# A gathered-row stream whose planner cost per half-step goes from 1.65 to 1.9

## The chip, the cores and the metric

The kernel runs on one core of a Trainium2 chip. The metric is the device time of one execution in microseconds (us); the median of the runs is compared. The program is one launch; its arrays are laid out on the host beforehand.

## The reference, cut to what matters

One layer of a streaming encoder is applied to 1024 prompt frames and to 32 frames of a running stream. After a mixer (attention and a recurrence) comes PEER, a retrieval of single-neuron experts:

```
q    = x @ w_q                            # 8 heads, two halves each
e    = top-16 of 16384 experts per head   # from two top-16 lists of 128 keys
gate = softmax(the 16 scores)
hid  = gelu(down[e] . x)                  # 8 heads x 16 experts = 128 per frame
y    = x + sum over the 128 of gate * hid * up[e]
out  = rmsnorm(y)
```

So every frame needs 128 rows of `down` and 128 rows of `up`, each of 1024 floats, chosen by its own data.

## The kernel before

The frames are cut into tiles of 128: tiles 0 to 7 of the prompt and a tile "S" of the 32 stream frames. The experts are computed in two ways.

The **dense way** takes tiles 0 to 4 (640 frames). It computes all 16384 experts as matrix products: 128 blocks of 128 experts, called e here. `hidden(e)` multiplies a block of `down` (line 261 to 263, three partial products for precision, in two chunks of 320 columns), ScalarE applies the gelu, VectorE multiplies by the gates (`gated`, L1211, from a matrix that the stream `scatter` has written to DRAM) and splits the product into a high and a low part (`vwl`, L255). The products with `up` follow four blocks later; VectorE adds their results into `acc` (L1274). The loop of `stage_v` has 128 steps, each with one `hidden` and `gated` (of the block four ahead) and two blocks of columns of the product with `up`.

The **row way** takes tiles 5, 6, "S" and 7 in this order, in the stream `rows`. For each of 128 + 128 + 32 + 128 = 416 columns of chosen experts, GpSimd starts a gather of 128 rows of 2048 floats, 1 MB, into one of five buffers (L1044); VectorE multiplies by x and sums (L1047); ScalarE does the gelu and the gate on one number per frame (L1049, L1050); VectorE adds gate times `up` row onto a PSUM tile (L1031). A tile ends with a norm and a store.

The two ways, and the streams `attn`, `routing` (the top-16 searches and gates) and `scatter`, are Python generators that emit instructions. **The weave** of their instructions is made by a planner at the end of `step_kernel`: each stream has a clock, and the stream with the lowest clock emits next and moves its clock on by what it yields. `rows` yields `GC` twice for each column, `stage_v` a fixed cost for each step:

```python
                late.append((k, row))
                yield GC
                if len(late) > 1:
                    add(*late.pop(0))
                yield GC
...
                    yield 6 * KD * n / 2400.        # stage_v, one step: n = 640, KD = 8
```

`v_start`, which opens the pools of the row stream, costs 10 x 1.0 for transposes and 6 x `3 * KD * NV / 2400.` for the first six `hidden` ahead of `stage_v`, whose own first six yields are 1.0 each. While the dense stage runs, the planner also sets a limit on how far ahead of the dense stream the rows may be put on VectorE (`PACED`, `AHEADS = dict(rows=60.0)`; `marks` holds, for each planner call of the dense stream, its clock and its last VectorE instruction):

```python
        if PHASE[0] in PACED.get(x[0], ()):
            due = x[2] - AHEADS.get(x[0], 0.0)
            hold = next((m for v, m in reversed(marks) if v <= due), None)
        with tc.issue_after(hold) if hold else nullcontext():
```

Within a stretch that is held in this way, a VectorE instruction of the row stream stands behind the VectorE instruction `hold` in VectorE's order; GpSimd's and ScalarE's are not held by it. The order that the planner writes is a priority: the framework that orders each engine's queue may still put an instruction that is ready ahead of an earlier one that isn't, within the dependencies and the holds. Each engine then works through its queue in order.

Of the kernel before, what the change touches and what calls it, by code (L numbers as in the profile page):

```python
# [50 lines left out]

GE = 6

GC, SC = 1.65, 1.0

PACED = dict(rows=(1, 2), routing=(0, 1, 2))
AHEADS = dict(rows=60.0)
# [1390 lines left out]
```

## Time and profile before

| | |
|---|---|
| median of 3 runs | 3603.99 us (3594.76 to 3604.02) |
| the profiled execution | 3604.3 us |
| its span, first to last instruction | 3602.5 us |
| TensorE matmuls busy | 3259.8 us (90%) |
| TensorE weight loads busy | 3135.7 us (87%) |
| VectorE busy | 2834.6 us (79%) |
| ScalarE busy | 1614.2 us (45%) |
| GpSimd busy | 2018.5 us (56%) |
| mean granted TensorE clock | 0.952 of full |

In the profile PE is TensorE, PEld its weight loads, DVE is VectorE, ACT ScalarE, POOL GpSimd, SP the queue that starts plain DMAs; L1047 is line 1047 of the kernel. Matmuls are pipelined and their ends are modelled, so counts of matmuls per stretch say more than their busy time. A mean of one instruction is in ns, all other times in us from the start of the span.

### The profile page before, as it was taken

Reading aid. Unit: us, or ns where it says so; the run is one execution under the profiler, and the core shown is the slowest. Engines: PE = TensorE matmul, PEld = TensorE weight load, DVE = VectorE, ACT = ScalarE, POOL = GpSimd, SP = SyncE. Lnnn points to the kernel's source line nnn. Section 1 sums busy time; section 2 is a strip of 40 time slices with the busy share of each in tenths; the row PEclk is TensorE's granted clock in tenths of the full one; section 3 lists DMA queues with packets and bytes.
Section 4 is the critical chain, followed back from the end, with each engine's and each line's share of the span. In section 5 each row is a group of like instructions: output and inputs, shape, how many; then the busy total and the mean of one; then the engine's idle time right before and its main releaser. Section 6 shows DMA issues by size and latency. Waiting matters only on the chain.

```text
span 3602.5 us, 60487 instructions
## 1 busy us (share of the span) xinstructions
PE 3259.8 (90%) x21635; PEld 3135.7 (87%) x21635; DVE 2834.6 (79%) x6148; ACT 1614.2 (45%) x4034; POOL 2018.5 (56%) x1339
## 2 busy tenths in 40 slices
PE   7999899989988888774899888999999999999997
PEld 6989899877877887774899888999999999999997
DVE  3354468898678999988999999888888888788833
ACT  3544344456777747763333333333333333333322
POOL 2322224546334556565666569666766676677633
PEclk9999999999988999886999999999999999999999
DMA  4554364444565635489888778999889898999832
GB/s 163 167 159 149 109 206 167 158 138 149 173 191 161 227 123 153 139 321 343 307 318 323 299 269 312 356 338 359 314 324 355 300 355 324 346 336 351 298 109 94
DMA packets 357453, 881.01 MB, mean 245 GB/s; under 512 B 31008, under 2 KB 190240, under 8 KB 299808
## 3 DMA queue, kind: packets, MB, share of 16 engines
q1 hardware_dynamic: 297248, 440.91, 36.9%
q0 software_dynamic: 59904, 436.23, 31.8%
q8 instruction: 171, 2.80, 0.3%
q14 instruction: 130, 1.06, 0.1%
HBM read 784.47 MB, written 92.14 MB: 243 GB/s over the span
## 4 chain that ended last, share of the span: by engine, by line
PE 57%; DVE 28%; DMA 4%; issue 4%; ACT 3%; POOL 2%; SPq 0%; DVEq 0%; ACTq 0%; POOLq 0%
PE gv L261 12%; PE gv L262 11%; PE gv L263 11%; PE gm L261 6%; PE gm L263 6%; PE gm L262 6%; DVE row L1047 5%; DVE xp L1031 5%; DVE acc L1274 2%; DVE oh L967 2%; PE ws L1093 1%; DVE ohB L1132 1%; DVE ef L972 1%; PE gb L468 1%; DMA row<-in_p_rows_dram,ei 1%
## 5 line engine op out<-in xcount | busy, mean ns | idle before, releaser
L261 PE MATMUL gv<-vwh,uh 128*128 128x320 f32 x2048 | 648.3, 317 | 96.7 <-DVE acc L1274 63.9
L255 POOL TENSOR_TENSOR wl<-wr,wh 128x1024 fp32r<-128x1024 f32 x160 | 390.4, 2453 | 540.7 <-ACT wh L254 524.9
L261 PE MATMUL gv<-vxh,dh 128*128 128x320 f32 x2048 | 643.9, 315 | 21.7 <-DVE acc L1274 10.2
L1044 POOL DMA_INDIRECT row<-in_p_rows_dram,ei x384 | 514.3, 1339 | 259.1 <-DVE xp L1031 141.7
L263 PE MATMUL gv<-vxh,dl 128*128 128x320 f32 x2048 | 639.8, 313 | 8.7 <-POOL dl L255 8.7
L262 PE MATMUL gv<-vwl,uh 128*128 128x320 f32 x2048 | 640.8, 313 | 0.0
L262 PE MATMUL gv<-vxl,dh 128*128 128x320 f32 x2048 | 639.7, 313 | 0.0
L263 PE MATMUL gv<-vwh,ul 128*128 128x320 f32 x2048 | 638.3, 313 | 0.5 <-POOL ul L255 0.5
L1047 DVE CUSTOM_DVE_ANT_0 row<-row,xg 128x1024 f32<-128x1024 f32 x416 | 599.4, 1441 | 3.1 <-DMA row<-in_p_rows_dram,ei 2.1
L1031 DVE SCALAR_TENSOR_TENSOR xp<-row,hid,xp 128x1024 f32<-128x1024 f32 x412 | 528.4, 1283 | 78.8 <-ACT hid L1050 77.0
L261 PEld LDWEIGHTS gv<-vwh,uh 128*128 128x128 f32 x2048 | 391.9, 191 | 111.6 <-DVE acc L1274 76.7
L255 POOL TENSOR_TENSOR dl<-dr,dh 128x512 fp32r<-128x512 f32 x256 | 361.3, 1415 | 201.4 <-ACT dh L254 193.4
L255 POOL TENSOR_TENSOR ul<-ur,uh 128x512 fp32r<-128x512 f32 x256 | 368.0, 1438 | 181.6 <-ACT uh L254 162.3
L261 PEld LDWEIGHTS gv<-vxh,dh 128*128 128x128 f32 x2048 | 392.0, 191 | 28.2 <-DVE vwl L255 13.1
L263 PEld LDWEIGHTS gv<-vxh,dl 128*128 128x128 f32 x2048 | 391.5, 191 | 9.5 <-POOL dl L255 9.5
L262 PEld LDWEIGHTS gv<-vwl,uh 128*128 128x128 f32 x2048 | 392.5, 192 | 0.0
L263 PEld LDWEIGHTS gv<-vwh,ul 128*128 128x128 f32 x2048 | 391.5, 192 | 0.9 <-POOL ul L255 0.9
L262 PEld LDWEIGHTS gv<-vxl,dh 128*128 128x128 f32 x2048 | 392.1, 191 | 0.0
L1135 POOL TENSOR_TENSOR ohB<-ohB,tr 128x512 f32<-128x512 f32 x160 | 200.0, 1256 | 262.4 <-DVE ohB L1132 216.8
L1274 DVE TENSOR_TENSOR acc<-acc,gv 128x320 f32<-128x320 f32 x496 | 235.4, 479 | 93.5 <-PE gv L263 90.2
L1049 ACT ACTIVATE hid<-hid 128x1 f32<-128x1 f32 x416 | 82.9, 199 | 486.5 <-DVE hid L1047 482.1
L254 ACT ACTIVATE uh<-ur 128x512 fp32r<-128x512 f32 x256 | 161.2, 630 | 301.3 <-PE gv L262 209.3
(324 smaller groups left out, 7520.7 us busy)
## 6 DMA issues: line engine op xcount, KB each, us to landing
dr<-in_p_downT_dram SPq DMA_DIRECT2D x256, 256.0 KB
ur<-in_p_up_dram SPq DMA_DIRECT2D x256, 256.0 KB
wr<-in_w_in_dram SPq DMA_DIRECT2D x88, 512.0 KB
W_d<-stg SPq DMA_DIRECT2D x40, 1024.0 KB
gw<-W_d SPq DMA_DIRECT2D x32, 1280.0 KB
wr<-in_p_wq_dram SPq DMA_DIRECT2D x48, 512.0 KB
wr<-in_w_out_dram SPq DMA_DIRECT2D x24, 512.0 KB
wr<-in_w_a_dram SPq DMA_DIRECT2D x12, 512.0 KB
```

The costliest lines, as they stand in the source:

```text
L254: A.activation(h, src, AF.Copy)
L255: (lo_engine or G).tensor_tensor(out=l, in0=src, in1=h.bitcast(F32), op=OP.subtract)
L261: PE.matmul(out, lh, rh, start=(i == 0), stop=False)
L262: PE.matmul(out, lh, rl, start=False, stop=False)
L263: PE.matmul(out, ll, rh, start=False, stop=(i == n - 1))
L967: V.tensor_tensor(out=oh[:T], in0=cf[:T, h].unsqueeze(2).to_broadcast([T, 16, NCAND]), in1=iota_c[:T].unsqueeze(1).to_broadcast([T, 16, NC ...
L1031: V.scalar_tensor_tensor(out=acc, in0=row[:, D:], scalar=hid[:, k:k + 1], in1=acc if k else first, op0=OP.mult, op1=OP.add)
L1044: G.indirect_dma_start(out=row, out_offset=None, in_=p_rows, in_offset=bass.IndirectOffsetOnAxis(ap=ei[:, k:k + 1], axis=0))
L1047: V.tensor_tensor_reduce(out=row[:, 0:D], in0=row[:, 0:D], in1=xt, scale=1.0, scalar=0.0, op0=OP.mult, op1=OP.add, accum_out=h)
L1049: A.activation(h, h, AF.Gelu)
L1135: G.tensor_tensor(out=bm, in0=bm, op=OP.mult, in1=tr[:, 2, xs].unsqueeze(2).to_broadcast([128, 4, 128]))
L1274: V.tensor_add(acc[:, db, cs], acc[:, db, cs], ps[:, :CHUNK])
```

## The change

One constant, the planner cost that the row stream yields twice for each column of gathered rows:

```diff
@@ -51,7 +51,7 @@
 
 GE = 6
 
-GC, SC = 1.65, 1.0
+GC, SC = 1.9, 1.0
 
 PACED = dict(rows=(1, 2), routing=(0, 1, 2))
 AHEADS = dict(rows=60.0)
```

A column costs 3.8 on the row stream's clock in place of 3.3. No instruction, buffer or transfer is added or removed; what can move is the place of the row stream's instructions among those of the other streams in each engine's queue.

## Rows read from the trace of the kernel before

**Rows 1.** The page: busy shares, and tenths in 40 slices of the span.
```profile
PE 3259.8 (90%) x21635; PEld 3135.7 (87%) x21635; DVE 2834.6 (79%) x6148; ACT 1614.2 (45%) x4034; POOL 2018.5 (56%) x1339
...
PE   7999899989988888774899888999999999999997
...
DVE  3354468898678999988999999888888888788833
```

**Rows 2.** Windows, three stretches: length, busy (instructions) per engine, clock, DMA, GB/s.
```profile
core 0: us, PE busy (x) PEld busy (x) DVE busy (x) ACT busy (x) POOL busy (x), PEclk, DMA share, GB/s
1684.00:2272.00 588.00, 524.13 (x3346) 514.43 (x3346) 580.27 (x1247) 206.09 (x551) 412.81 (x286) 0.94 0.83 305
2272.00:3421.00 1149.00, 1126.87 (x7590) 1117.21 (x7589) 951.45 (x1443) 427.45 (x1153) 790.97 (x572) 0.99 0.90 335
3421.00:3602.50 181.50, 160.12 (x1096) 158.82 (x1094) 65.08 (x135) 47.95 (x103) 66.47 (x51) 0.95 0.30 102
```

**Rows 3.** Waits of PE in 1684 to 2272: total, times, longest.
```profile
PE gv L261 <- DVE acc L1274: 51.1, 20, 6.6
PE gv L261 <- DVE vwl L255: 7.3, 5, 2.4
PE gv L261 <- ACT uh L254: 3.5, 3, 2.1
```

**Rows 4.** Chain that ended last, 1684 to 2272, by line.
```profile
by line: DVE row L1047 22.6%; DVE xp L1031 18.4%; DVE acc L1274 6.7%; issue 6.2%; PE gv L261 6.0%; PE gv L263 5.4%; PE gv L262 5.4%; DVE gv L1211 3.2%; DVE oh L967 3.0%; DVE vwl L255 2.8%; DMA row<-in_p_rows_dram,ei 2.6%; DVE ef L972 2.5%; 
```

**Rows 5.** DVE groups in 1684 to 2272: busy, mean ns, idle before.
```profile
L1047 DVE CUSTOM_DVE_ANT_0 row<-row,xg 128x1024 f32<-128x1024 f32 x123 | 193.8, 1577 | 1.1 <-DMA row<-in_p_rows_dram,ei 1.1
L1031 DVE SCALAR_TENSOR_TENSOR xp<-row,hid,xp 128x1024 f32<-128x1024 f32 x123 | 156.8, 1275 | 0.8 <-ACT hid L1050 0.8
...
L1047 DVE DVE_READ_ACCUMULATOR2_ANT hid<- 128x1 f32 x123 | 9.4, 76 | 0.0
```

**Rows 6.** Waits of PE in 2272 to 3421.
```profile
PE gv L261 <- DVE acc L1274: 20.4, 20, 3.5
PE gv L261 <- DVE vwl L255: 1.3, 6, 0.4
```

**Rows 7.** Windows of line L1047 from 0 on; each column of rows counts twice.
```profile
0.00:1684.00 1684.00, 45.07 (x66) 0.93 0.54 177
0.00:1730.40 1730.40, 59.51 (x86) 0.93 0.55 181
0.00:1799.00 1799.00, 83.94 (x114) 0.93 0.56 185
...
0.00:1991.50 1991.50, 146.66 (x199) 0.93 0.59 198
0.00:2131.00 2131.00, 197.81 (x256) 0.93 0.60 205
0.00:2272.00 2272.00, 239.95 (x312) 0.93 0.62 210
...
0.00:3207.00 3207.00, 535.48 (x733) 0.95 0.70 247
```

**Rows 8.** Windows of DVE on the tile vwl from 0 on; each block e counts twice.
```profile
0.00:1684.00 1684.00, 4.84 (x10) 0.93 0.54 177
0.00:1730.40 1730.40, 6.50 (x13) 0.93 0.55 181
0.00:1799.00 1799.00, 10.12 (x21) 0.93 0.56 185
...
0.00:1991.50 1991.50, 20.85 (x44) 0.93 0.59 198
0.00:2131.00 2131.00, 28.16 (x60) 0.93 0.60 205
0.00:2272.00 2272.00, 35.98 (x77) 0.93 0.62 210
...
0.00:3207.00 3207.00, 96.24 (x207) 0.95 0.70 247
```

**Rows 9.** Timeline of DVE, 1668 to 1682.
```profile
1668.63 1.22 DVE L1047 CUSTOM_DVE_ANT_0 row<-row,xg 128x1024 f32<-128x1024 f32 x1
1669.77 0.08 DVE L1047 DVE_READ_ACCUMULATOR2_ANT hid<- 128x1 f32 x1
1670.45 1.29 DVE L1031 SCALAR_TENSOR_TENSOR xp<-row,hid,xp 128x1024 f32<-128x1024 f32 x1 [0.60 <-ACT hid L1050]
1671.65 1.22 DVE L1047 CUSTOM_DVE_ANT_0 row<-row,xg 128x1024 f32<-128x1024 f32 x1
...
1678.15 3.58 DVE L1211 TENSOR_TENSOR early<-early,gw 128x320 f32<-128x320 f32 x6
```

**Rows 10.** Tile row: duration min/median/max in ns, first and last start.
```profile
L1047 DVE CUSTOM_DVE_ANT_0 row<-row,xg x416: 1192/1219/4628, 1537.8 to 3421.3; 128x1024 f32<-128x1024 f32 x139
L1031 DVE SCALAR_TENSOR_TENSOR xp<-row,hid,xp x412: 1259/1284/1292, 1551.4 to 3423.1; 128x1024 f32<-128x1024 f32 x138
```

**Rows 11.** DVE groups in 2272 to 3421.
```profile
L1047 DVE CUSTOM_DVE_ANT_0 row<-row,xg 128x1024 f32<-128x1024 f32 x259 | 359.5, 1388 | 1.7 <-DMA row<-in_p_rows_dram,es 0.8 <-DMA row<-in_p_rows_dram,ei 0.8
```

## The prediction

> **What bounds the kernel now.** The page comes first [rows 1]: TensorE has 90% of the span and VectorE 79%, so shares alone don't tell which of them to relieve. The tenths do: from slice 20 to slice 25 (about 1710 to 2250 us) VectorE shows 9 throughout and TensorE 8 and 9; then VectorE falls to 8 and TensorE stays at 9; in the last three slices VectorE drops to 8, 3 and 3. The row stream lives in these slices, from 1537.8 to 3423.1 us [rows 10], so I cut its life into three stretches with windows [rows 2].
>
> In 1684 to 2272 VectorE is busy 580.3 of 588 us: it is full. TensorE does 3346 matmuls there. In 2272 to 3421 it does 7590 in 1149 us, 151 ns each, with VectorE idle for 1149 - 951 = 198 us. At 151 ns the 3346 would have taken 507 us, so the first stretch lost 81 us. The waits say to whom: 51.1 + 7.3 us of TensorE's waiting there ended with a VectorE instruction [rows 3], and the chain of waits runs 41% through the two row instructions of VectorE, L1047 and L1031 [rows 4]. In the second stretch the same wait is 20.4 + 1.3 us in twice the time [rows 6]: TensorE sets the pace. In the third VectorE is idle for 116 of 181.5 us [rows 2].
>
> So a row instruction has three prices: its full length ahead of 2272, next to nothing between 2272 and 3421, nothing in the tail as long as the rows end ahead of the dense products.
>
> **What the constant does.** Nothing is removed or added: 416 gathers, 416 of L1047 and of L1031 remain. What moves is their place in VectorE's queue, and two things in the code set it: the clock, and the limit of 60 units. I count the dense clock from the first call of `stage_v`. Block e is emitted at v(e) = 6 + 12.8 (e - 4) for e of 6 and more, since a step costs 6 x 8 x 640 / 2400 = 12.8. The row stream starts when `v_start` opens its pool, 10 x 1.0 + 6 x 6.4 = 48.4 earlier. Column k starts at -48.4 + 2 GC (k - 1), and 4 more for each finished tile; it must stand behind block e's last VectorE instruction (`vwl`) once its clock less 60 has reached v(e). So ahead of block e there can be at most (v(e) + 108.4 - 4 per finished tile) / (2 GC) + 1 columns.
>
> Does the limit bind today? The windows of L1047 and of `vwl`, which end at the same times, count both [rows 7, 8]. At the end of block 6 (1730.4 us) 43 columns stand ahead and the limit is 43; block 10 (1799): 57 of 58; block 22 (1991.5): 100 of 105; block 30 (2131): 128 of 136; block 38 (2272): 156 of 166. So it binds at first and then the rows fall behind it by themselves: from 2272 to 3207 us, blocks 38 to 103, they make 210.5 columns in 65 steps, 3.24 a step, where the clock would let 12.8 / 3.3 = 3.88 pass.
>
> With GC at 1.9 the limits are 37, 51, 91, 118 and 144 in the same places: below the count of today at each one, by 6, 6, 9, 10 and 12. The rows must come later, whatever the ordering would like. At block 103 the limit is 361 against 366.5 seen, and its pace, 12.8 / 3.8 = 3.37 a step, is above the 3.24 that the rows reach by themselves. So the new limit decides in the early stretch and the rows' own pace later.
>
> **The sum.** Up to 1684 us 33 columns are done [rows 7]; with five blocks' `vwl` past by then [rows 8], the limit ahead of block 5 (v = 5) becomes 30, from 35. Those 3 ran while VectorE had nothing else, waiting for gates that came at 1678 [rows 9]: there they cost nothing, and now they come later. That is a loss, and it is in the count: between 1684 and 2272 there are 156 - 33 = 123 columns now and 144 - 30 = 114 after, 9 fewer. One costs 1.577 + 0.076 + 1.275 = 2.93 us of VectorE there [rows 5], so 26.4 us leave the full stretch.
>
> How much of it becomes time? VectorE's idle time is 7.7 us, so from that side nearly all. TensorE's lost 81 us are 58 us of waits on VectorE, 72%; the rest is other waits and a granted clock of 0.94 against 0.99 [rows 2]. So the stretch shortens by 19 us (72%) to 26 us (all); I take 22, nearer the middle than either, since a full engine is relieved but part of what TensorE loses isn't its doing. From below, nothing excludes 0, if TensorE meets another wait at once; from above 26 is not the end either (third rival).
>
> The 12 columns that block 38 no longer has ahead of it must go somewhere. At 3.24 a step the remaining 416 - 144 = 272 take 84 steps, to block 122; a step takes (3207 - 2272) / 65 = 14.4 us, so the last column comes at 2272 - 22 + 84 x 14.4 = 3460 us, where it was 3421 [rows 10]. Block 127 comes at 2250 + 89 x 14.4 = 3532, and four steps without a `hidden` follow. So the rows still end some 70 us ahead of the last block, under a TensorE that has the say. Cost 0; without that cover each column would cost the 3.02 us from one L1047 to the next where rows run alone [rows 9].
>
> GpSimd's gathers move with the buffers: a gather waits for the L1031 that frees one of five. SP's queue holds almost nothing of the row stream (an input, a norm weight and a store for each of four tiles). No wait is added but the hold, and what is queued behind a held row instruction on VectorE is the rows after it and `acc` and `vwl` of later steps, for which TensorE waits if the row stands too far ahead (second rival).
>
> Sum: 3604.3 (the profiled execution, 0.3 above the median) - 22 = **3582 us**.
>
> L1047 reads two SBUF operands and lasts 1.58 us on average in the full stretch [rows 5], 1.39 us in the next [rows 11] and 1.19 us at its shortest [rows 10]. The Trainium skill, SBUF — State Buffer, section Summary: rules for kernel authors, says that a VectorE instruction with two SBUF inputs and a GpSimd instruction that reads SBUF block each other fully, whichever starts second. By that rule the columns that leave may have been cheap or dear ones: nine at the shortest length would be 9 x 2.54 = 23 us, an estimate, in place of 26; the trace agrees that the length varies, and the mean carries the sum.
>
> **The rivals.**
>
> 1. *No change that can be measured*: the rows leave, but TensorE stops for something else in the early stretch (its `uh` split on ScalarE, 3.5 us of waits today [rows 3], or the products with gates in lock-step with its own `hidden`). For it: the stretch is a chain through several engines, and only 41% of it are row instructions [rows 4]; 41% of 26 us is 11 us. Against it: the other waits are small. 3593 to 3604 us.
>
> 2. *Slower through a worse queue later on*: with the limit near the rows' own pace, columns collect behind a block's `vwl` and run one after another once it is past, with `acc` of the next products behind them. The price is at most one L1031 or L1047 (1.3 us) for each of the 89 blocks after 2272, 115 us; it decides against me from 22 / 89 = 0.25 us a block. For it: `acc` is what TensorE waits for already [rows 6]. Against it: VectorE has 17% spare there, and the same limit bound up to block 10 without harm that shows. At 0.45 us a block it gives 3604 - 22 + 40 = 3622 us.
>
> 3. *A larger gain through the clock*: the granted clock is 0.94 in the full stretch. Of the two levels, 1.2 and 2.4 GHz, that is 12% of 588 us at the lower one, 71 us, in which half the work, 35 us, is lost; at 0.99 it would be 6 us. If TensorE's pauses are what pulls it down, up to 29 us come on top: 3553 us. Against it: only a third of the waits would go. The Trainium skill, TensorE: Matmul & The Clock Gate, section HAM oscillation, says that idle gaps bring the slow clock back; the trace agrees as far as the stretch with the waits has the lower clock.
>
> 4. *Slower through the end*: the rows run out past the dense products. That needs their pace to fall under 272 / 91 = 3.0 a step. At 2.8 some 17 columns are left at the last product, 17 x 3.02 = 51 us and some 10 us of norm and store, less the dense tail of about 24 us that runs beside them: 3582 + 37 = 3619 us. For it: with a later clock the rows give way to every dense instruction. Against it: in the early stretch they were ahead of their clock and still made (156 - 43) / 32 = 3.5 a step [rows 7, 8].
>
> **How the numbers follow.** Forecast (3578 to 3592) 0.50, first rival 0.20, second 0.13, third 0.10, fourth 0.07. The predicted time is the forecast's, 3582. What a measurement can tell from no change is about 0.3%, 11 us. Faster by more than that: 0.50 + 0.10 = 0.60; within: 0.20; slower: 0.20. The range leaves out half of the slower cases and the far end of the third: 3555 to 3612 us.
>
> **What would show it.** In the changed trace: 37, 51 and 144 columns or fewer ahead of blocks 6, 10 and 38; a VectorE in the early stretch that is still over 95% busy, with block 38 near 2250 us; TensorE's waits for `acc` there at 35 us or less; the same 14.4 us a step after it; the last L1031 near 3460 us. The prediction is wrong if block 38 comes no earlier though fewer rows stand ahead of it (then rows weren't the price), if the steps after it take 14.6 us or more, or if L1031 is still running when the last `acc` is done.

## The result, and the profile after

The changed kernel takes 3660.69 us (median of 4, 3651.90 to 3667.82) beside 3604.01 of the kernel before: 1.0161 times its time, 95% interval 1.0136 to 1.0186, so 57 us slower where 22 us faster was forecast. Its profiled execution took 3667.82 us, with a span of 3666.1 us (before: 3604.3 and 3602.5).

Where the time went is read from windows over the same stretches as [rows 2], with the second one cut at 2900. First the kernel after, then the two halves of the second stretch before:

```profile
core 0: us, PE busy (x) PEld busy (x) DVE busy (x) ACT busy (x) POOL busy (x), PEclk, DMA share, GB/s
1684.00:2272.00 588.00, 517.02 (x3238) 506.63 (x3238) 552.80 (x1204) 198.45 (x522) 391.11 (x273) 0.91 0.79 286
2272.00:2900.00 628.00, 586.35 (x3878) 580.14 (x3878) 483.48 (x740) 223.51 (x594) 399.75 (x297) 0.97 0.87 319
2900.00:3421.00 521.00, 502.32 (x3395) 497.46 (x3394) 433.29 (x656) 192.83 (x521) 360.18 (x260) 1.00 0.91 339
```

```profile
2272.00:2900.00 628.00, 618.27 (x4175) 613.13 (x4174) 522.63 (x793) 232.57 (x623) 427.02 (x312) 1.00 0.90 335
2900.00:3421.00 521.00, 508.61 (x3417) 504.08 (x3416) 428.81 (x651) 194.88 (x530) 363.95 (x261) 0.99 0.89 334
```

Count TensorE's matmuls. In 1684 to 2272 there are 108 fewer than before; at 588 / 3346 = 176 ns each that is 19 us of work not yet done. In 2272 to 2900 there are 297 fewer, at 150 ns, 45 us; after that 22, 3 us. The sum, 67 us, is the 63.6 us of the two spans but for what comes later. So two thirds of the loss lie in the stretch for which the prediction had a cost of 0.

The 45 us split by the same rows. TensorE stands still for 628 - 586.35 = 41.7 us (9.7 before); the share of the 9.7 that belongs to 3878 matmuls is 9.0, so 32.6 us are new. A matmul is busy for 151.2 ns in place of 148.1, 12.0 us over 3878. Together 44.6.

The second part goes with the clock: the granted clock is 0.97 in this stretch and was 1.00, and of the two levels, 1.2 and 2.4 GHz, the upper one is the one granted nearly throughout before. The Trainium skill, TensorE: Matmul & The Clock Gate, section HAM oscillation, says that pauses between matmuls bring the slow clock back; the trace agrees so far as the stretch that got the pauses also got the lower clock, and the early stretch went from 0.94 to 0.91.

Who lets TensorE stand? The waits of the two engines after, first in 1684 to 2272 and then in 2272 to 3421:

```profile
PE gv L261 <- DVE acc L1274: 58.3, 18, 7.2
...
PE gv L261 <- DVE acc L1274: 57.4, 28, 7.5
```
```profile
DVE acc L1274 <- PE gv L263: 117.4, 125, 1.4
DVE gv L1211 <- ACT gv L1169: 49.8, 38, 3.1
DVE xp L1031 <- ACT hid L1050: 22.2, 43, 2.0
DVE row L1047 <- DMA row<-in_p_rows_dram,ei: 17.2, 9, 4.7
```

and VectorE's waits of before in 2272 to 3421:

```profile
DVE gv L1211 <- ACT gv L1169: 76.4, 86, 2.5
DVE xp L1031 <- ACT hid L1050: 62.5, 129, 2.2
DVE acc L1274 <- PE gv L263: 38.3, 55, 1.7
```

TensorE's wait for `acc` went from 20.4 us [rows 6] to 57.4, and its longest from 3.5 to 7.5 us; in the early stretch it didn't fall to 35 us or less but rose, from 51.1 [rows 3] to 58.3. At the same time VectorE waits for TensorE ahead of `acc` three times as long as before (117.4 us for 38.3): the two engines now wait for each other. And VectorE, the engine that was to be relieved, is idle in 1684 to 2272 for 588 - 552.8 = 35.2 us, where it was 7.7.

The work did leave the early stretch as worked out. VectorE's groups there after:

```profile
L1047 DVE CUSTOM_DVE_ANT_0 row<-row,xg 128x1024 f32<-128x1024 f32 x114 | 175.0, 1544 | 6.0 <-DMA row<-in_p_rows_dram,ei 5.9
L1031 DVE SCALAR_TENSOR_TENSOR xp<-row,hid,xp 128x1024 f32<-128x1024 f32 x113 | 144.0, 1274 | 0.0
```

114 columns where there were 123 [rows 5], 9 fewer. Nothing came of it. VectorE stands 27.5 us longer there, and the largest part is a wait of another stream: the routing's search (L900) waits for its scores (`scl`), for which no wait stands in this stretch before:

```profile
DVE sv L900 <- DMA scl<-sc: 11.8, 4, 6.1
```

**Where the limit stands.** The code of the planner takes as `hold` the last VectorE instruction of a dense call (`new[-1]`). The prediction had this as the block's `vwl`. In the trace, once the products with `up` run, the last one of a step is the step's fourth `acc` (L1274); step s, in which block s + 4 is emitted, ends with number 4 (s - 3). The limit on columns ahead of it is the prediction's formula with v = 6 + 12.8 s (and 47.4 for the start of the row clock in place of 48.4: the row stream can first emit after the first yield of `v_start`, so that 9 x 1.0 + 6 x 6.4 are left). Windows of L1047 and of L1274 after, from 0 up to just behind the last `acc` of the steps 10, 20, 34, 60 and 100 (each column counts twice in L1047):

```profile
0.00:1850.30 1850.30, 94.95 (x128) 0.93 0.56 186
...
0.00:2033.20 2033.20, 148.53 (x196) 0.93 0.58 195
...
0.00:2272.35 2272.35, 217.22 (x288) 0.92 0.60 204
...
0.00:2683.70 2683.70, 332.61 (x462) 0.93 0.64 222
0.00:3280.15 3280.15, 523.29 (x726) 0.94 0.69 242
```
```profile
0.00:1850.30 1850.30, 12.65 (x28) 0.93 0.56 186
...
0.00:2272.35 2272.35, 57.30 (x124) 0.92 0.60 204
```

and L1047 before, at the last `acc` of the steps 10, 34, 60 and 100:

```profile
0.00:1847.55 1847.55, 99.25 (x136) 0.93 0.57 189
...
0.00:2255.55 2255.55, 234.24 (x304) 0.93 0.61 209
...
0.00:2634.45 2634.45, 357.83 (x478) 0.94 0.66 229
0.00:3219.85 3219.85, 537.00 (x736) 0.95 0.70 248
```

| step | before: columns, limit | after: columns, limit |
|---|---|---|
| 10 | 68, 74 | 64, 64 |
| 20 | 102, 112 | 98, 98 |
| 34 | 152, 166 | 144, 144 |
| 60 | 239, 265 | 231, 231 |
| 100 | 368, 416 | 363, 364 |

Counted in this way at every step from 4 to 127, the rows before never come nearer than 4 columns to the limit until they run out. After, they are within one column of it at 109 of the 111 steps that end before the last column is done, the late ones among them. (At every fourth step they are up to 3 past it: there the `acc` that was emitted last, the hold, runs two places ahead of the step's end.) The 119 of 124 in an expectation below goes by 49.05 and counts the steps after the last column too; in that count the kernel before has 14.

**What a held row does.** VectorE's timeline after, from step 44:

```profile
2428.66 0.50 DVE L1211 TENSOR_TENSOR gv<-gv,gw 128x320 f32<-128x320 f32 x1 [1.62 <-ACT gv L1169]
2429.53 0.49 DVE L1274 TENSOR_TENSOR acc<-acc,gv 128x320 f32<-128x320 f32 x1 [0.36 <-PE gv L263]
...
2431.28 0.49 DVE L1274 TENSOR_TENSOR acc<-acc,gv 128x320 f32<-128x320 f32 x1 [0.87 <-PE gv L263]
2433.04 0.49 DVE L1274 TENSOR_TENSOR acc<-acc,gv 128x320 f32<-128x320 f32 x1 [1.27 <-PE gv L263]
2434.51 0.49 DVE L1274 TENSOR_TENSOR acc<-acc,gv 128x320 f32<-128x320 f32 x1 [0.98 <-PE gv L263]
2434.91 1.22 DVE L1047 CUSTOM_DVE_ANT_0 row<-row,xg 128x1024 f32<-128x1024 f32 x1
```

VectorE stands and waits for each of a step's four `acc`, at the pace at which TensorE makes them, since no row may go between; then the rows come in a run. And some 20 us ahead of it:

```profile
2407.56 0.49 DVE L1274 TENSOR_TENSOR acc<-acc,gv 128x320 f32<-128x320 f32 x1 [0.50 <-PE gv L263]
2407.97 1.22 DVE L1047 CUSTOM_DVE_ANT_0 row<-row,xg 128x1024 f32<-128x1024 f32 x1
2409.11 0.08 DVE L1047 DVE_READ_ACCUMULATOR2_ANT hid<- 128x1 f32 x1
2409.11 1.28 DVE L1031 SCALAR_TENSOR_TENSOR xp<-row,hid,xp 128x1024 f32<-128x1024 f32 x1
2415.13 1.23 DVE L1047 CUSTOM_DVE_ANT_0 row<-row,xg 128x1024 f32<-128x1024 f32 x1 [4.73 <-DMA row<-in_p_rows_dram,ei]
2416.28 0.08 DVE L1047 DVE_READ_ACCUMULATOR2_ANT hid<- 128x1 f32 x1
2416.28 0.48 DVE L1274 TENSOR_TENSOR acc<-acc,gv 128x320 f32<-128x320 f32 x1
```

An `acc` is queued behind a row whose gather is late. No `acc` runs between 2407.56 and 2416.28, and TensorE, which waits for it, starts no matmul from 2408.97 on for 7.8 us. Behind this stop the granted clock is 0.76 (2416.8 to 2424 us, 38 matmuls in 7.2 us), where it was 1.00 ahead of it (2395 to 2409 us, 98 in 14.0). The issues of DMA between 2398 and 2418 (count, KB each, median us to landing) show what runs beside the late gather, two loads of gates:

```profile
gw<-W_d SPq DMA_DIRECT2D x2, 1280.0 KB, 14.1
...
row<-in_p_rows_dram,ei POOLq DMA_INDIRECT x5, 12.5
```

The five gathers land after 12.5 us, where the median over 2272 to 2900 is 8.2. Of the gaps between starts of successive matmuls in 2272 to 3421, those with more than 1.5 us above the usual 0.15 sum to 45 us after (13 of them) and to 10 us before (5).

### The profile page after: what moved, and what is told of

Its sections match the earlier page's. It is cut to its first block, busy times and chain, and to the rows that moved or that the text cites. A ratio compares the mean times of both kernels' runs of the same rounds, so it can differ in the third digit from the quotient of the medians.

```text
span 3666.1 us, 60449 instructions
## 1 busy us (share of the span) xinstructions
PE 3280.1 (89%) x21635; PEld 3152.5 (86%) x21635; DVE 2827.2 (77%) x6148; ACT 1619.1 (44%) x4034; POOL 2005.7 (55%) x1339
## 4 chain that ended last, share of the span: by engine, by line
PE 58%; DVE 24%; DMA 8%; issue 5%; ACT 3%; POOL 2%; SPq 0%; DVEq 0%; ACTq 0%; POOLq 0%
PE gv L261 12%; PE gv L262 12%; PE gv L263 12%; PE gm L261 6%; PE gm L263 6%; PE gm L262 6%; DVE row L1047 4%; DVE xp L1031 4%; DMA row<-in_p_rows_dram,ei 3%; PE ws L1093 2%; DVE ohB L1132 1%; DVE oh L967 1%; DVE acc L1274 1%; DVE ef L972 1%; DMA W_d<-stg 1%
## 5 line engine op out<-in xcount | busy, mean ns | idle before, releaser
L261 PE MATMUL gv<-vxh,dh 128*128 128x320 f32 x2048 | 646.0, 316 | 20.3 <-DVE acc L1274 8.7
L1047 DVE CUSTOM_DVE_ANT_0 row<-row,xg 128x1024 f32<-128x1024 f32 x416 | 596.4, 1441 | 30.6 <-DMA row<-in_p_rows_dram,ei 23.3
L1031 DVE SCALAR_TENSOR_TENSOR xp<-row,hid,xp 128x1024 f32<-128x1024 f32 x412 | 527.2, 1280 | 38.3 <-ACT hid L1050 36.0
L255 POOL TENSOR_TENSOR dl<-dr,dh 128x512 fp32r<-128x512 f32 x256 | 353.8, 1387 | 167.8 <-ACT dh L254 154.0
L1274 DVE TENSOR_TENSOR acc<-acc,gv 128x320 f32<-128x320 f32 x496 | 234.3, 479 | 173.0 <-PE gv L263 170.8
```

Source lines behind the costliest of these rows:

```text
L255: (lo_engine or G).tensor_tensor(out=l, in0=src, in1=h.bitcast(F32), op=OP.subtract)
L261: PE.matmul(out, lh, rh, start=(i == 0), stop=False)
L1031: V.scalar_tensor_tensor(out=acc, in0=row[:, D:], scalar=hid[:, k:k + 1], in1=acc if k else first, op0=OP.mult, op1=OP.add)
L1047: V.tensor_tensor_reduce(out=row[:, 0:D], in0=row[:, 0:D], in1=xt, scale=1.0, scalar=0.0, op0=OP.mult, op1=OP.add, accum_out=h)
L1274: V.tensor_add(acc[:, db, cs], acc[:, db, cs], ps[:, :CHUNK])
```

## The experiments

Theory: the limit, now reached at every step, is the price, and the clock `GC` matters only through it. Rivals: the later clock itself makes the order worse; gathers that land late; VectorE's lost time. All ratios are against the kernel before on the same chip (medians 3604.0 to 3605.0 us).

| run | GC, limit | median us | ratio, 95% | block 38 at, us | blocks 38 to 119, us |
|---|---|---|---|---|---|
| before | 1.65, 60 | 3604 | 1 | 2272 | 1165 |
| after | 1.9, 60 | 3660.69 | 1.0136 to 1.0186 | 2293 | 1209 |
| e1_late_free | 1.9, 200 | 3607.74 | 1.0008 to 1.0028 | 2279 | 1159 |
| e2_early_tight | 1.65, 0 | 3591.74 | 0.9952 to 0.9980 | 2263 | 1162 |
| e3_early_free | 1.65, 200 | 3609.32 | 1.0003 to 1.0022 | 2293 | 1158 |
| e4_late_loose | 1.9, 80 | 3627.17 | 1.0051 to 1.0085 | 2277 | 1186 |
| e5_hold_early | 1.9, 60 then 200 | 3616.76 | 1.0018 to 1.0047 | 2288 | 1160 |
| e6_hold_late | 1.9, 200 then 60 | 3661.86 | 1.0138 to 1.0172 | 2289 | 1209 |
| e7_half_late | 1.9, 60, half gathers | 3660.57 | 1.0136 to 1.0185 | 2247 | 1246 |
| e8_half_early | 1.65, 60, half gathers | 3706.88 | 1.0264 to 1.0298 | 2259 | 1286 |
| e9_start_held | 1.65, -40 then 200 | 3593.19 | 0.9951 to 0.9979 | 2259 | 1171 |
| e10_tighter | 1.65, -30 | 3589.24 | 0.9934 to 0.9967 | 2260 | 1169 |
| e11_later_free | 2.3, 1000 | 3614.41 | 1.0008 to 1.0032 | 2292 | 1159 |
| e12_short_held | 1.9, 60, short L1031 | 3548.21 | 0.9827 to 0.9860 | 2237 | 1149 |
| e13_short_free | 1.9, 200, short L1031 | 3562.71 | 0.9867 to 0.9900 | 2251 | 1146 |
| e14_short_tight | 2.0, 60, short L1031 | 3597.03 | 0.9965 to 0.9987 | 2243 | 1187 |

The last two columns are from the profiled execution: the start of the block's second `vwl`. Where no limit acts late (e1, e3, e5, e11) blocks 38 to 119 take 1158 to 1160 us; in e2, e9 and e10, which are one program (see below), 1162, 1171 and 1169. The time of block 38 varies more: e1 and e11, also one program, differ by 13 us there and by 7 in the median. A difference of that size between two rows of the table says nothing.

**The limit or the clock.** e1_late_free, e2_early_tight, e3_early_free and e4_late_loose:

```diff
 GC, SC = 1.9, 1.0             # e1, e4; 1.65 in e2, e3
-AHEADS = dict(rows=60.0)
+AHEADS = dict(rows=200.0)     # e1, e3; 0.0 in e2; 80.0 in e4
```

> The cost per half-column stays at the changed 1.9, but the limit is widened from 60 to 200 units, so that no column of rows is held (36.8 columns more are allowed at each step, and the trace of before stands at most 27 columns above the changed limit). The limit as the cause: the rows go back to the pace that they find by themselves (46 columns by the last acc of step 4, about 135 by that of step 30), TensorE's waits for acc in 2300 to 2900 us fall from 34 to about 12 us, and the time is that of the kernel before, 3595 to 3612 us. The clock itself as the cause (rows later in the planner's order and so behind every dense instruction in priority, limit or not): the time stays at 3650 to 3670 us.

> The cost stays at the 1.65 of before, the limit is narrowed from 60 to 0 units, which takes 18 columns from what is allowed ahead of each step's last acc: it should bind from step 4 (33 allowed, 46 done before) to about step 45 and then let go. The limit as the cause: slower although the clock is that of before, by 20 to 45 us (the changed kernel lost some 32 us up to block 47 and 60 by block 95): 3625 to 3650 us, with columns equal to the limit up to about step 45. The clock itself as the cause: 3595 to 3612 us, as before.

> The cost of before, 1.65, with the limit widened to 200 units. In the trace of before no step's last acc has fewer than 3 columns of room, so the limit decided only at the first steps. The limit as the cause: the same as before within 0.3%, 3594 to 3612 us. If the limit of before was of use (it keeps the first rows from standing ahead of the first dense products), slower by 5 to 20 us.

> The changed cost, 1.9, with the limit widened by a third, to 80 units: 5.3 columns more are allowed at each step, which puts the limit within 2 to 4 columns of where the rows of before stood by themselves. The limit as the cause: between the two kernels, 3610 to 3645 us, with columns equal to the limit in some of the steps and not in all as in the changed kernel (119 of 124 within one column). The clock itself as the cause: 3650 to 3670 us.

With the new clock and no limit in reach the loss is gone: 3607.74 us, 53 us under the changed kernel. With 80 in place of 60 the rows are within one column of the limit at 74 of the 111 steps ahead of the last column, and 27 us of the late stretch's 50 (1209 less 1159) are there: dose and loss go together. e2 missed its expectation, which was slower: it is 12 us faster. In its trace the limit acts only on the first steps (15 columns ahead of the first `vwl`, not 29); after them it is 3 columns away or more, so it wasn't the late hold that it was meant to be; its gain is told of below.

**Early or late.** e5_hold_early and e6_hold_late change the limit at a row clock of 1500:

```diff
-            due = x[2] - AHEADS.get(x[0], 0.0)
+            ahead = AHEADS.get(x[0], 0.0)
+            if x[0] == "rows":
+                ahead = 60.0 if x[2] < SWITCH else 200.0    # e5; 200 then 60 in e6
+            due = x[2] - ahead
```

with `SWITCH = 1500.0` and the clock at 1.9.

> The changed cost 1.9 with the limit of 60 units up to clock 1500 on the planner's own scale (about step 39 of the dense stage) and of 200, which binds nowhere, after it. Two stretches are priced apart: the changed kernel lost 21 us up to block 38 and 37 us more up to block 79. If the limit costs in each stretch what it costs in the changed kernel: 3604 + 21 = 3625 us (3615 to 3635), and the steps after block 47 are as long as before. If the early loss is given back later (rows that are late have room where VectorE is idle): 3600 to 3612 us.

> The counterpart: the limit of 200 units up to clock 1500, of 60 after it. If the limit costs in each stretch what it costs in the changed kernel: 3604 + 37 = 3641 us (3630 to 3650), with block 38 near 2275 us. If the late loss is only the after-effect of a late start, 3600 to 3615 us.

The late hold alone gives the whole loss (3661.86, 1209 us from block 38 to 119), more than the 3630 to 3650 that were expected. The early one alone is 2 to 9 us above the three kernels without a limit in reach (3607.74, 3609.32, 3614.41); its time lies in the range in which each stretch has a price of its own, but the two prices, 12 and 57 us over the kernel before, add up to more than the 57 of both holds. So the early hold neither gained the 22 us nor cost much. It does bring the wait of the routing's search (9.9 us in e5, none in e1, e3 and e6).

**The clock alone, further.**

```diff
-GC, SC = 1.65, 1.0
+GC, SC = 2.3, 1.0
-AHEADS = dict(rows=60.0)
+AHEADS = dict(rows=1000.0)
```

> The row stream's clock alone, made slower still: 2.3 per half-column, 4.6 a column, 2.78 columns a step by the clock, and a limit of 1000 units that binds nowhere. By its clock the stream would end beyond the dense stage. If the clock only gives a priority and the rows go by their own pace where nothing holds them: 3600 to 3612 us, some 3.2 columns a step. If a later clock by itself delays the rows: they run out past the last product, 3625 us or more.

The order is that of e1 on every engine, instruction for instruction: this is the same program, and its 2 us over the expected range are less than the 7 by which the two medians of it differ. e3, at 1.65, has the same order on VectorE up to 3296 us, near the end of the rows. Where nothing is held, the row clock decides nothing from 1.9 to 2.3, and next to nothing at 1.65.

**Bytes.** e7_half_late (clock 1.9) and e8_half_early (1.65) gather 512 KB a column and use the same half for both row instructions:

```diff
-                G.indirect_dma_start(out=row, out_offset=None, in_=p_rows,
+                G.indirect_dma_start(out=row[:, 0:D], out_offset=None, in_=p_rows.rearrange("e (a d) -> (e a) d", a=2),
...
-                    V.scalar_tensor_tensor(out=acc, in0=row[:, D:], scalar=hid[:, k:k + 1],
+                    V.scalar_tensor_tensor(out=acc, in0=row[:, 0:D], scalar=hid[:, k:k + 1],
```

> The changed cost 1.9 and limit 60, but each gather brings 512 KB in place of 1 MB: rows of 1024 floats are gathered, and the sum uses the same half again in place of the row of up (that part of the computation is left out). Read against the same edit at 1.65. If the held rows cost time because their gathers start late and land late (20 us of VectorE's waits for gathers in 2300 to 2900 us, 1 us before), the difference between the two halves shrinks to 30 us or less, from 57. If they cost time because VectorE stands still at the held rows for TensorE's products and TensorE then for VectorE, it stays at 45 to 65 us.

> The cost 1.65 and limit 60 of before with the gathers halved in the same way (the row of up is left out of the computation). The reference for the other half run. VectorE's work is unchanged and TensorE sets the pace after block 38, so by VectorE as the bound of the early stretch 3585 to 3605 us; if the gathers' bytes bound the early stretch or the wait for the gates ahead of it (the gates land among gathers at 417 GB/s), 3560 to 3585 us.

Half the bytes (DMA share 0.63 in 2272 to 2900, a gather lands in 5.2 us) did not lift the loss: within one column of the limit at all 111 steps ahead of the last column, 1246 us from block 38 to 119, and matmul gaps of over 1.5 us that sum to 71 us. The largest, 6.7 us, falls on the end of a tile and holds a wait for a gather of 1.8 us. At those of 4.9 us `acc` stands behind two columns that were there to be run, with little or no wait for a gather (VectorE in e7, at one of them):

```profile
2553.45 0.49 DVE L1274 TENSOR_TENSOR acc<-acc,gv 128x320 f32<-128x320 f32 x1 [0.55 <-PE gv L263]
2553.85 1.28 DVE L1031 SCALAR_TENSOR_TENSOR xp<-row,hid,xp 128x1024 f32<-128x1024 f32 x1
2555.04 1.22 DVE L1047 CUSTOM_DVE_ANT_0 row<-row,xg 128x1024 f32<-128x1024 f32 x1
...
2556.19 1.28 DVE L1031 SCALAR_TENSOR_TENSOR xp<-row,hid,xp 128x1024 f32<-128x1024 f32 x1
2557.38 2.07 DVE L1047 CUSTOM_DVE_ANT_0 row<-row,xg 128x1024 f32<-128x1024 f32 x1
...
2559.39 0.48 DVE L1274 TENSOR_TENSOR acc<-acc,gv 128x320 f32<-128x320 f32 x1
```

So a late gather makes a stop longer where it meets one; it isn't needed for it. e8 missed by over 100 us: with shorter gathers its rows run up to the limit even at 1.65 (within one column at 60 of the 95 steps ahead of the last column, from about step 40 on, at the limit's own 3.88 a step), and it loses more than the changed kernel. All kernels that reach the limit late (after, e4, e6, e7, e8, e14) take longer there than any that doesn't, 1186 to 1286 us for 1146 to 1171, at either clock. How shorter gathers alone would do without a limit wasn't tried, so the pair has no measure of its own, and e7 less e8 says nothing of the question they were made for.

**VectorE's time or the order.** e12_short_held, e13_short_free and e14_short_tight cut the multiply-add:

```diff
+                    w = D if k == 0 else 128
-                    V.scalar_tensor_tensor(out=acc, in0=row[:, D:], scalar=hid[:, k:k + 1],
-                                           in1=acc if k else first, op0=OP.mult, op1=OP.add)
+                    V.scalar_tensor_tensor(out=acc[:, 0:w], in0=row[:, D:D + w], scalar=hid[:, k:k + 1],
+                                           in1=acc[:, 0:w] if k else first, op0=OP.mult, op1=OP.add)
```

> The changed kernel (1.9, limit 60), with the multiply-add of each column (L1031) cut to 128 of its 1024 elements from the second column of a tile on, so that this part of the output is left out. It takes some 1 us a column, 3.4 us a step, off VectorE and nothing off the hold. If the price of the hold is VectorE's time (it stands idle up to the step's last acc and then lacks the time for its rows before the next products arrive), the price goes: this kernel is within 15 us of the one with the limit at 200 that runs beside it, and under 3615 us. If the price is in the order itself (rows ahead of acc that wait for a late gather, products that wait for acc whatever VectorE still has to do), it stays at least 35 us above it, near 3640 us.

> The same short multiply-add with the limit at 200, where nothing is held: the measure for the run beside it. Both theories expect 3560 to 3605 us: with whole instructions it took 3608 us, and VectorE is full only up to block 38, where some 100 us of its work now go.

e12 came out faster than e13, which looks like VectorE's time. But its rows reach the limit up to about step 29 only; after that they stay 2 to 13 columns short of it, and there it says nothing. Its 14 us over e13 are there at block 6 already (1723 us against 1741). So a lower limit:

> The short multiply-add again (128 of 1024 elements, that part of the output left out), with the clock at 2.0 and the limit at 60, so that the limit (some 348 columns at step 100, where the two kernels with the short instruction had 353 and 356) is below the rows all along and not up to step 34 only. If the price of the hold is VectorE's time, the steps stay under 14.2 us each between blocks 38 and 119 (14.0 and 14.1 in the two others) and the whole is under 3580 us. If the price is in the order itself (rows ahead of acc that wait for a gather, products that wait for acc), the steps take 14.6 us or more there, and the whole is over 3600 us.

Now the rows are within one column of the limit at all 118 steps ahead of the last column, and the late stretch takes 1187 us for 1146: 41 us, where the whole instruction had 50. A step takes 14.65 us (1187 / 81), past the 14.6 that was set for the order itself; the total, 3597, lies between the two bounds. The window of 2272 to 2900 in e14 and in e13, and then TensorE's waits in 2272 to 3421 in e14 and in e13 (their lines are numbered one higher):

```profile
2272.00:2900.00 628.00, 603.00 (x4050) 598.79 (x4049) 396.38 (x760) 227.49 (x613) 412.27 (x305) 0.99 0.87 322
```
```profile
2272.00:2900.00 628.00, 620.45 (x4212) 617.01 (x4211) 403.13 (x795) 232.32 (x630) 416.51 (x313) 1.00 0.89 327
```
```profile
PE gv L261 <- DVE acc L1275: 28.2, 19, 3.8
```
```profile
PE gv L261 <- DVE acc L1275: 11.6, 20, 0.6
```

VectorE is busy 63% of the time there (396.38 of 628) and TensorE still stops for it, now for up to 3.8 us where it was 0.6. So in the late stretch most of the price isn't a lack of time on VectorE; it is the order: an `acc` queued behind rows that were bunched by the hold.

**The start.** e9_start_held (same edit as e5, with -40 below a row clock of 1060, 200 above, clock 1.65) and e10_tighter follow e2's gain:

```diff
-AHEADS = dict(rows=60.0)
+AHEADS = dict(rows=-30.0)     # e10
```

> The cost of before, 1.65; the limit is -40 units up to clock 1060 of the planner's scale (about step 5 of the dense stage) and 200, which binds nowhere, after it. With the limit at 0 throughout, block 0's vwl stood behind 15 columns in place of 29 and came 24 us sooner, block 6 came 34 us sooner, and 10 us were left at the end. If the gain comes from the start alone (fewer gathers beside the load of the gates): 3570 to 3592 us, since after the start nothing is held. If the limit of 0 gained by a bound on the rows in the early stretch: 3592 to 3605 us.

> The cost of before with the limit at -30 units throughout: 9 columns fewer than with the limit at 0, where the smallest room was 3 columns from step 4 to 13, so it binds from step 4 to about step 25 and then lets go. If a limit that binds in the early stretch costs 10 to 15 us there (as between the runs at 1.9 with and without it), slower than the run with the limit at 0 (3592) by that: 3592 to 3606 us. If fewer rows in the early stretch are what counts: 3570 to 3590 us.

Neither is a new experiment: e2, e9 and e10 have the same instructions in the same order on every engine. The stream with the lowest clock emits next, and `marks` holds only the dense calls already emitted, so a limit below 0 finds the mark that 0 finds; e10's limit is no tighter than e2's, and never binds at steps 4 to 25. That e9, which is free from step 5 on, is the same program too shows that a limit of 0 acts at the start alone. So this is one kernel, measured three times with 3591.74, 3593.19 and 3589.24 us, 12 to 16 us faster than before and the fastest with nothing left out.

It has 15 columns ahead of the first `vwl` instructions in place of 29, and these come at 1640 to 1644 us in place of 1667, block 6's 29 to 34 us earlier. By block 38 it is 9 to 13 us, and at block 127 still 7 to 13. What comes sooner can be read from the chain of work that ended last, as start and time to landing: a store of the gates before, the same store in e2, and in e2 the load of the gates' second half:

```profile
1630.70 16.81 DMA W_d<-stg
...
1625.96 5.06 DMA W_d<-stg
...
1641.39 5.80 DMA gw<-W_d
```

Before, the same load was started at 1657.90 us, 16.5 later. Why more than half of the gain goes again in between isn't settled.

## Why the prediction was wrong, point by point

- *What bounds the kernel* holds: with the short multiply-add and no limit (e13 against e1) blocks 6 to 38 take 510 us for 545, and blocks 38 to 119 only 13 us less. VectorE is the dear engine early.
- *The work that leaves*: 9 columns and 26.4 us were forecast, 9 columns left and VectorE is busy for 27.5 us less (580.3 less 552.8). Right. One reading under it is not: in [rows 9] VectorE does not wait for gates. No wait stands at the line of 1678.15; rows stood ahead of it in the queue. And the first six `vwl` of [rows 8] are the first halves of blocks 0 to 5, so at 1684 four blocks were done and not five. Neither changes the count.
- *How much of it becomes time* was sized at 72% to all. None did: VectorE's idle time grew by 27.5 us, 11.8 of them the routing's wait, and TensorE's waits for `acc` by 7. Even without a hold the share was too high: between blocks 6 and 38 e13 has 103 columns that are 1275 - 346 = 929 ns shorter, 96 us of a full engine, and gained 35 us on e1 and 40 on e11, about 40%. At that rate the 22 us would have been 10; it is the average over 96 us, and what the first 26 alone are worth no run shows.
- *The step that failed* is "the new limit decides in the early stretch and the rows' own pace later". It put the limit against 3.24 columns a step, the pace of rows that were free, and took the hold for a `vwl` that comes early in its step. The hold is the step's last `acc`, so rows wait for TensorE's products; and the limit, which from the first steps on is below the place where the rows stood before, never lets them go. The prediction compared the two paces; its own two places at block 103, 361 allowed and 366.5 seen, say that rows which are held at the limit from the start are still held there. Counts of 37 and 144 were right at block 6 and step 34; at the `vwl` of blocks 10 and 38 there were 53 and 149, for 51 and 144, since a `vwl` is not where the limit is set.
- *The cost of 0 after 2272* was the dear term: 14.9 us a step (1209 / 81) for 14.4. The prediction named 14.6 as the bound that would refute it.
- *Rival 2* had the mechanism, columns that collect and an `acc` behind them, and its price: 0.45 us a block against (1209 - 1165) / 81 = 0.54. It got 0.13. What stood against it, that the same limit bound up to block 10 without harm, was worth nothing: in the trace of before the rows are 4 columns or more short of it from step 4 on, where the holds on `acc` begin. Its sum, 3622, was low because it kept the 22 us of gain: 3604 + 44 + 21 of the early stretch is 3669, the profiled execution's 3667.8.
- *Rival 3*, the clock, went the other way: 0.91 for 0.94 in the early stretch, and 0.97 for 1.00 in 2272 to 2900. *Rival 4* didn't come: the last L1047 starts at 3500.4 us, 40 later than forecast, and still over 100 us ahead of block 127 (3615).

What stays open: how the late price divides between stops that a late gather lengthens and stops that the order makes alone, and the 9 us of it that may be VectorE's time; and how much of the 14 to 21 us by which block 38 is later (than in e1 and in before) is the change's doing, where two kernels of the same order differ by 13.

## What to carry to other kernels

Before you cost a limit on how far work may run ahead, find in the code the very instruction that it hangs on and what that one waits for, and count in the trace how far work stands from the limit at each step: a limit that is never reached is free, and one that is reached at every step ties two engines together. An engine that works through its queue in order turns a bunch of side work into stops of the main engine even with a third of its time to spare, so look at what stands ahead of the evacuation of PSUM, not at the busy share. Price a relief of a full engine by taking work out of it in an experiment: here a microsecond of VectorE was worth 0.4 on average, and nothing where a hold moved the work. And compare the order on every engine before two runs are called two experiments: five of these fourteen were two programs.

## What the hardware showed that was not expected

- With fewer gathers at the start other transfers landed sooner: with 15 gathered columns ahead of the first `vwl` in place of 29, a 1 MB store of the gates landed after 5.1 us in place of 16.8, and the load that follows the stores started 16.5 us earlier (e2 against before). VectorE multiplied by what that load brought 5.8 us after its start; before it was 20.3 us, at the end of them behind rows in VectorE's queue. With gathers of half the size (e8) the load started at 1633.7 us, 24.2 sooner, and block 6 came 28 us earlier. That the transfers share bandwidth with the gathers is a reading of these numbers, not measured by itself.
- Halving a transfer's bytes made the kernel of before 2.8% slower (e8), and its rows ran up to the limit, which was not in reach before. That the limit is the cause there too is not shown: half gathers without a limit were not run.
- A stop of 7.8 us of TensorE came from one gather that was late by 4.7 us: the rest is the row work that stood around it in VectorE's queue.
